# A hybrid decoder layer on one core: sums of weights' blocks moved in halves

## The chip, the cores and the metric

The kernel runs on one core of a Trainium2 chip. The metric is the device time of one execution in microseconds (us); less is better. Times come from repeated executions; the profile is of one of them.

## The reference

One decoder layer on 512 tokens of width 2048, in float32, cut to what matters:

```python
h = rmsnorm(x, g_pre)
q, k, v, z_att, u, g_glu, z_conv = split(h @ w_in, 7 * [1024])
y_att  = stick_breaking_attention(q, k, v) * silu(z_att)        # 8 heads of 128, causal
c = u * sigmoid(g_glu)
c = causal_depthwise_conv(c, conv_w, width=31) + conv_b
y_conv = (silu(layernorm(c)) @ w_pw2 + b_pw2) * silu(z_conv)
out = x + rmsnorm(concat(y_att, y_conv) @ w_out, g_post)
```

## The kernel before

Every product is made of three matmuls on parts: a float32 block is split on the chip into a rounded upper part (`h_...`, made by ScalarE, ACT) and a lower part (`l_...`, made by VectorE, DVE). The weights come from memory in blocks of one megabyte (`r_...`, two buffers), asked for on SyncE's queue (SP). TensorE (PE) follows an order written out by hand: a list of *steps*, each with one block of weights and mostly two *units* of 24 matmuls. The block of the next step is loaded while a step runs; its upper part, then its lower part, is made from it, and the lower part's end frees the buffer for another load.

The order of the steps, with the tiles' names: a prologue for the first gate columns (`gn`, in 16 blocks `n`); `u`, `q`, `k`, `g` of the first columns (steps 0 to 7); the values `v` (steps 8 to 21); the rest of `u`, `q`, `k`, `g`, with the attention heads in between, and the gates `za` (22 to 49); the gates `z` (50 to 63); the pointwise product `pw` (64 to 67); the output product `w` (68 to 95).

Three of the products, `v`, `z` and the output, use seven block products in place of eight. Four of the seven need a sum of blocks of the weights (5, 6, 7 and 4 in `SUMS`). These sums are not made on the chip's engines but in memory: `plan_sums` makes a list of transfers, each asked for on GpSimd's queue (POOL). For each sum two blocks per pair (`kg` 0 and 1; the output has two pairs `p`) are first copied into a tile in memory, out of the weights or out of an earlier finished sum (L528); then another block of the weights is added onto each by an accumulating transfer (L524). A block is 128 rows of 4 pieces of 2 KB. The tiles are `vs`, `zs` and `ws`. `v` and `z` have 16 transfers each, the output 32, 64 in all. SP later loads the finished sums like other weights.

The transfers are spread over the steps: `sum_next` takes the next of a list and ties it to the last matmul that was put down (`latest`), so it is not asked for before that matmul is done. POOL's queue is in order, so what stands behind a waiting request waits too. For `v`: one after every second block of the prologue from `n` 5 on, then one after each of three units of four. For `z` and the output together (`sumq`, the lists taken in turn): 1.5 a step from step 20 to 48, and again from step 64 on.

POOL also cuts off the future in the attention (`affine_select` on `t`, L698: four on each of two tiles per head, which the transposes `aT` wait for), clears the edge of `hg` (L401), adds up `ln_sum` and makes some products with gates. DVE makes the lower parts and, in the background, the 31 taps of the convolution (L410). ACT writes 16 pieces of prepared activations (`kept`) to memory for later.

Of the kernel before, what the change touches and what calls it, by code (L numbers as in the profile page):

```python
# [11 lines left out]
F32 = mybir.dt.float32  # L12
F32R = mybir.dt.float32r
AF = mybir.ActivationFunctionType
ALU = mybir.AluOpType

P = 128
S = 512
# [31 lines left out]
SUMS_FROM, SUMS_A_STEP = 20, 1.5  # L50
# [3 lines left out]
def hybrid_layer(  # L54
# [15 lines left out]
    nc = tc.nc  # L70
# [10 lines left out]
    dram = ctx.enter_context(tc.tile_pool(name="dram", bufs=1, space=bass.MemoryType.DRAM))  # L81
# [355 lines left out]
    def layer_norm():  # L437

        mu = mean_of(ln_sums[0], "mu")
        yield  # L440
        sqs = [late(f"ln_sq{c}") for c in range(CT)]
        for c in range(CT):
            nc.vector.tensor_tensor(out=conv[c], in0=conv[c], in1=mu, op=ALU.subtract)
            nc.scalar.activation(sqs[c], conv[c], AF.Square)
            if c >= 2:
                eng = nc.gpsimd if c % 2 == 0 else nc.vector
                eng.tensor_tensor(out=sqs[c % 2], in0=sqs[c % 2], in1=sqs[c], op=ALU.add)
            yield
        nc.vector.tensor_tensor(out=sqs[0], in0=sqs[0], in1=sqs[1], op=ALU.add)
        var = mean_of(sqs[0], "var")  # L450
        v, y, t = late("ln_v"), late("ln_y"), late("ln_t")
        nc.vector.tensor_scalar_add(v, var, LN_EPS)
        tc.keep_in_program_order(nc.scalar.preload_act_table_set(LN_EXP))
        rsqrt(y, v, t)
        yield
        for c in range(CT):
            nc.vector.tensor_tensor(out=conv[c], in0=conv[c], in1=y, op=ALU.mult)
            nc.scalar.activation(
                conv[c], conv[c], AF.Silu, scale=vec[:, c, V_LG : V_LG + 1],
                bias=vec[:, c, V_LB : V_LB + 1],  # L460
            )
            yield
        for c in range(CT):
            s_hi[c], s_lo[c] = late(f"s_hi{c}", F32R), t2(f"s_lo{c}", F32R)
            split(s_hi[c], s_lo[c], conv[c])
            yield
# [8 lines left out]
    def rows_first(ps, w, between):  # L475


        hi, lo = w
        parts = [h_at(i, 0, P) for i in range(4)]
        for n, (which, i) in enumerate(FIRST):  # L480
            a, b = {"hh": (0, hi), "hl": (0, lo), "lh": (1, hi)}[which]
            nc.tensor.matmul(
                ps, parts[i][a], b[:, i, :], start=n == 0, stop=False, skip_group_check=True
            )
            for f in between.get(n + 1, ()):
                f()

    def rows_block(kg, m, ps, w, between=()):

        hi, lo = w  # L490
        parts = [h_at(kg * 4 + i, m * P, (m + 1) * P) for i in range(4)]
        for i, (a, _) in enumerate(parts):
            nc.tensor.matmul(ps, a, hi[:, i, :], start=kg + i == 0, stop=False, skip_group_check=True)
            nc.tensor.matmul(ps, a, lo[:, i, :], start=False, stop=False, skip_group_check=True)
            if i == 0:
                for f in between:
                    f()
        for i, (_, a) in enumerate(parts):
            last = kg == 3 and i == 3
            latest[0] = nc.tensor.matmul(  # L500
                ps, a, hi[:, i, :], start=False, stop=last, skip_group_check=True
            ).ins
# [5 lines left out]

    SUMS = {5: ((0, 0), (0, 1)), 6: (5, (1, 1)), 4: (6, (1, 0)), 7: ((0, 1), (1, 1))}
    PLAIN = {1: (0, 0), 3: (1, 1), 2: (1, 0)}

    def plan_sums(name, order, pairs, block):

        made, todo = {}, deque()
        for q in order:
            base, more = SUMS[q]
            for accumulate in (False, True):
                for p in range(pairs):  # L520
                    for kg in range(2):
                        def go(q=q, base=base, more=more, accumulate=accumulate, p=p, kg=kg):
                            if accumulate:
                                return nc.gpsimd.dma_start(  # L524
                                    made[q, p, kg], block(*more, p, kg), accum_op=ALU.add
                                )
                            made[q, p, kg] = dram.tile([P, 4, S], F32, name=f"{name}{q}{p}{kg}")
                            return nc.gpsimd.dma_start(  # L528
                                made[q, p, kg],
                                made[base, p, kg] if isinstance(base, int)  # L530
                                else block(*base, p, kg),
                            )
                        todo.append(go)
        return made, todo

    def sum_next(todo):

        if todo:
            tc.add_manual_dep(
                todo.popleft()().ins, latest[0].name,  # L540
                mybir.DependencyInfo(mybir.DependencyClass.Sync, mybir.DependencyReason.DATA),
                reason="not before its step",
            )
# [12 lines left out]
    def v_w(r, c, p, kg):  # L556
        rows_ = slice((r * 2 + kg) * S, (r * 2 + kg + 1) * S)
        return w_in[rows_, C_V + c * S : C_V + (c + 1) * S].rearrange("(k p) c -> p k c", p=P)

    v_sum, v_sumq = plan_sums("vs", (5, 6, 7, 4), 1, v_w)  # L560
    v_form, v_ps, v_part = {}, {}, {}

# [404 lines left out]
    def load_final():  # L967
        for e in range(4):
            gp[e] = fin.tile([P, S], F32, tag="gp", bufs=4, name=f"gp{e}")
            nc.sync.dma_start(gp[e], g_post[e * S : (e + 1) * S].partition_broadcast(P))  # L970
# [243 lines left out]
    n_zc = len(steps)  # L1214
    gates_c()
    n_in = len(steps)
# [9 lines left out]
    with tc.manual_schedule(engines={mybir.EngineType.DVE, mybir.EngineType.Activation}):  # L1226
# [77 lines left out]
        def do(f, *args):  # L1304
            return partial(f, *args)
# [48 lines left out]
        for n, (kg, m) in enumerate(blocks):  # L1354
            if n == 0:
                rows_first(ps0[0], w0[0][1:], {8: [do(turn_block, 1)]})
            else:
                rows_block(
                    kg, m, ps0[m], w0[kg][1:], [do(turn_block, n + 1)] if n + 1 < len(blocks) else (),
                )  # L1360
            for f in plan[n]:
                f()
            if n + 1 < len(blocks):
                keeps[n + 1]()
            if n >= 5 and n % 2:
                sum_next(v_sumq)
        keep_rows(3)
        for _ in range(4):
# [36 lines left out]
    units_done, due = 0, 0  # L1405
    for n, step in enumerate(steps):
        if n == n_att:
            start.close()
            zp = att.enter_context(tc.tile_pool(name="zp", bufs=1, space=bass.MemoryType.PSUM))
            op = att.enter_context(tc.tile_pool(name="op", bufs=1, space=bass.MemoryType.PSUM))  # L1410
            attp = att.enter_context(tc.tile_pool(name="attp", bufs=1))
        if n == n_norm:
            att.close()
            conv_stack.close()
            op2 = ctx.enter_context(
                tc.tile_pool(name="op2", bufs=4, space=bass.MemoryType.PSUM)
            )
            late_stack = ExitStack()
            late_pool = late_stack.enter_context(tc.tile_pool(name="late", bufs=11))
            ln = layer_norm()  # L1420
            bgq.extend([lambda: next(ln, None)] * (3 * CT + 3))
        if n == n_pw - 1:
            make_form(ORDER[0])
        if n == n_pw:
            late_stack.close()
            fin = ctx.enter_context(tc.tile_pool(name="fin", bufs=1))
            load_final()
        if SUMS_FROM <= n < n_zc - 1 or n >= n_in:
            due += SUMS_A_STEP
        if n + 1 < len(steps) and n + 1 not in loaded:  # L1430
            loaded[n + 1] = steps[n + 1].load()
        w = loaded.pop(n)
        for unit in step.units:
            unit(w)
            units_done += 1
            if units_done % 4:
                sum_next(v_sumq)
            if due >= 1:
                sum_next(sumq)
                due -= 1  # L1440
            if n == 0 and unit is step.units[0]:
                turn_vectors()
            if n < n_norm:
                ticks[0] += 1
                next(heads_run)
                if n_v <= n < n_att:
                    background(1, LATER, weights_split[0])
                else:
                    background(4, LATER)
            else:  # L1450
                background(2, LATER)
# [28 lines left out]
```

## Time and profile before

| | |
|---|---|
| median of 3 runs | 857.09 us (856.87 to 857.32) |
| the profiled execution's own time, and its span | 858.71 us, 857.0 us |
| busy: PE, PEld, DVE, ACT, POOL | 847.6, 702.3, 658.5, 417.3, 137.6 us |
| DMA queue of SP (q1): MB, share of 16 engines | 120.74, 41.0% |
| DMA queue of POOL (q0): MB, share of 16 engines | 69.21, 33.7% |
| clock granted to PE | 0.998 |

The profile is taken inside one execution: the span runs from its first to its last instruction. PE is the matmul itself, PEld the load of its weights, which overlaps it. A matmul of 512 columns is listed with 0.39 us but the next starts 0.23 us after it, since they are pipelined; so short gaps do not show as idle. Where a row ends in brackets, the number is the engine's idle time before it, and behind the arrow stands what ended it. A DMA's time runs from the request to its landing.

### The profile page before, as it was taken

To read this page: it belongs to the slowest core of one execution; us is meant where nothing else is said; L and a number is where in the kernel's file an instruction comes from. 1 tells how busy PE (TensorE), PEld (TensorE's weight loads), DVE (VectorE), ACT (ScalarE), POOL (GpSimd) and SP (SyncE) were. 2 spreads that over 40 slices of the span, in tenths; PEclk is the share of its full clock that TensorE was granted. 3 is DMA by queue.
4 is the path that set the end of the run, shared out by engine and by line. 5 is a ranking of instruction groups with operands and counts; after the bars stand their busy time and mean duration, and the time that the engine had idled before them with its cause. 6 is when DMAs were issued, how large, how long until landed. Compare 5 with 4: busy or idle time off the path is not lost.

```text
span 857.0 us, 9935 instructions
## 1 busy us (share of the span) xinstructions
PE 847.6 (99%) x3872; PEld 702.3 (82%) x3872; DVE 658.5 (77%) x791; ACT 417.3 (49%) x475; POOL 137.6 (16%) x170
## 2 busy tenths in 40 slices
PE   9999999999999999999999999999999999999996
PEld 7888878888888888888888888888888888888885
DVE  5698899777589798997969898468964776458774
ACT  6784222565534342436432535369843356455543
POOL 0111110010130223222121333330000100000031
PEclk9999999999999999999999999999999999999999
DMA  8798989575877879876689887937755995557783
GB/s 317 243 289 196 325 256 234 191 225 196 299 229 209 245 148 215 276 197 196 191 222 188 235 245 159 283 103 289 295 197 197 220 263 205 197 197 260 288 282 102
DMA packets 92278, 195.04 MB, mean 228 GB/s; under 512 B 3702, under 2 KB 46210, under 8 KB 86856
## 3 DMA queue, kind: packets, MB, share of 16 engines
q1 hardware_dynamic: 66688, 120.74, 41.0%
q0 software_dynamic: 22304, 69.21, 33.7%
q10 hardware_dynamic: 3240, 4.46, 1.5%
q8 instruction: 30, 0.49, 0.2%
q14 instruction: 16, 0.13, 0.0%
HBM read 186.01 MB, written 75.50 MB: 305 GB/s over the span
## 4 chain that ended last, share of the span: by engine, by line
PE 91%; DMA 4%; DVE 2%; ACT 2%; issue 0%; POOL 0%; ACTq 0%; DVEq 0%; POOLq 0%
PE za L351 3%; PE za L353 3%; PE a L1089 3%; PE za L352 3%; PE a L1090 3%; PE a L1091 3%; PE k L353 3%; PE k L351 3%; PE k L352 3%; PE u L351 3%; PE u L353 3%; PE u L352 3%; PE q L353 3%; PE q L351 3%; PE q L352 3%; DMA r_q<-in_w_in_dram 2%
## 5 line engine op out<-in xcount | busy, mean ns | idle before, releaser
L410 DVE SCALAR_TENSOR_TENSOR acc<-hg,vec,acc 128x512 f32<-128x512 f32 x240 | 183.1, 763 | 7.2
L105 DVE TENSOR_TENSOR l_w<-r_w,h_w 128x2048 fp32r<-128x2048 f32 x28 | 64.2, 2292 | 43.5 <-ACT h_w L104 43.5
L104 ACT ACTIVATE h_w<-r_w 128x2048 fp32r<-128x2048 f32 x28 | 53.6, 1916 | 43.4 <-DMA r_w<-ws 16.9
L353 PE MATMUL k<-h_hi,l_k 128*128 128x512 f32 x128 | 50.0, 390 | 1.1 <-DVE l_k L105 1.1
L351 PE MATMUL u<-h_hi,h_u 128*128 128x512 f32 x128 | 50.1, 392 | 0.0
L351 PE MATMUL q<-h_hi,h_q 128*128 128x512 f32 x128 | 50.1, 392 | 0.0
L351 PE MATMUL za<-h_hi,h_za 128*128 128x512 f32 x128 | 50.1, 391 | 0.0
L351 PE MATMUL k<-h_hi,h_k 128*128 128x512 f32 x128 | 50.1, 391 | 0.0
L353 PE MATMUL q<-h_hi,l_q 128*128 128x512 f32 x128 | 49.9, 390 | 0.0
L353 PE MATMUL za<-h_hi,l_za 128*128 128x512 f32 x128 | 49.9, 390 | 0.0
L353 PE MATMUL u<-h_hi,l_u 128*128 128x512 f32 x128 | 49.9, 390 | 0.0
L352 PE MATMUL u<-h_lo,h_u 128*128 128x512 f32 x128 | 49.8, 389 | 0.0
L352 PE MATMUL za<-h_lo,h_za 128*128 128x512 f32 x128 | 49.8, 389 | 0.0
L352 PE MATMUL q<-h_lo,h_q 128*128 128x512 f32 x128 | 49.8, 389 | 0.0
L352 PE MATMUL k<-h_lo,h_k 128*128 128x512 f32 x128 | 49.8, 389 | 0.0
L1091 PE MATMUL a<-h_w,f_lo 128*128 128x512 f32 x128 | 49.8, 389 | 0.0
L1089 PE MATMUL a<-h_w,f_hi 128*128 128x512 f32 x128 | 49.8, 389 | 0.0
L1090 PE MATMUL a<-l_w,f_hi 128*128 128x512 f32 x128 | 49.8, 389 | 0.0
L105 DVE TENSOR_TENSOR l_z<-r_z,h_z 128x2048 fp32r<-128x2048 f32 x14 | 32.1, 2291 | 16.3 <-ACT h_z L104 16.3
L105 DVE TENSOR_TENSOR l_v<-r_v,h_v 128x2048 fp32r<-128x2048 f32 x14 | 32.1, 2290 | 15.3 <-ACT h_v L104 15.3
L698 POOL TENSOR_SCALAR_AFFINE_SELECT t<-t 128x128 f32<-128x128 f32 x64 | 33.6, 562 | 54.1 <-ACT t L734 30.1
L104 ACT ACTIVATE h_v<-r_v 128x2048 fp32r<-128x2048 f32 x14 | 26.8, 1916 | 29.6 <-PE g L352 13.2
(381 smaller groups left out, 2238.2 us busy)
## 6 DMA issues: line engine op xcount, KB each, us to landing
ws<-in_w_out_dram POOLq DMA_DIRECT2D x24, 1024.0 KB, 9.4
r_w<-ws SPq DMA_DIRECT2D x16, 1024.0 KB
vs<-in_w_in_dram POOLq DMA_DIRECT2D x12, 1024.0 KB, 12.7
zs<-in_w_in_dram POOLq DMA_DIRECT2D x12, 1024.0 KB, 9.3
r_w<-in_w_out_dram SPq DMA_DIRECT2D x12, 1024.0 KB
r_u<-in_w_in_dram SPq DMA_DIRECT2D x8, 1024.0 KB
r_q<-in_w_in_dram SPq DMA_DIRECT2D x8, 1024.0 KB
r_k<-in_w_in_dram SPq DMA_DIRECT2D x8, 1024.0 KB
```

The costliest lines, as they stand in the source:

```text
L104: nc.scalar.activation(hi, src, AF.Copy)
L105: made = nc.vector.tensor_tensor(out=lo, in0=src, in1=f32(hi), op=ALU.subtract)
L351: nc.tensor.matmul(ps, wh, ah, start=first, stop=False)
L352: nc.tensor.matmul(ps, wh, al, start=False, stop=False)
L353: latest[0] = nc.tensor.matmul(ps, wl, ah, start=False, stop=last).ins
L410: bgq.append(lambda j=j: nc.vector.scalar_tensor_tensor(out=acc, in0=hg[:, j : j + S], scalar=vec[:, ct, j : j + 1], in1=acc, op0=ALU.mult ...
L698: nc.gpsimd.affine_select(out=blk, in_=blk, compare_op=ALU.is_gt, fill=0.0, base=0, pattern=[[-1, P]], channel_multiplier=1,)
L1089: nc.tensor.matmul(ps, fh[:, kk, ts], hi[:, k, :], start=st, stop=False, skip_group_check=True)
L1090: nc.tensor.matmul(ps, fh[:, kk, ts], lo[:, k, :], start=False, stop=False, skip_group_check=True)
L1091: nc.tensor.matmul(ps, fl[:, kk, ts], hi[:, k, :], start=False, stop=en, skip_group_check=True)
```

## The change

Each transfer that makes sums of weights moves half a block (two of the four pieces of each row), so there are 128 in place of 64; a copy and the addition onto it are halved alike, and a tile is made with its first half. They are asked for twice as often: for `v`, after each block of the prologue from 5 on (11 halves, where there were 6 wholes), then two after the first unit and one after the second, in turn; for `z` and the output, 1.5 halves a unit in place of 1.5 blocks a step. The bytes are the same, the loads of the finished sums as well, and no other line differs.

```diff
-                    for kg in range(2):
-                        def go(q=q, base=base, more=more, accumulate=accumulate, p=p, kg=kg):
+                    for kg, half in ((0, 0), (0, 1), (1, 0), (1, 1)):
+                        def go(q=q, base=base, more=more, accumulate=accumulate, p=p, kg=kg, half=half):
+                            ks = slice(2 * half, 2 * half + 2)
                             if accumulate:
                                 return nc.gpsimd.dma_start(
-                                    made[q, p, kg], block(*more, p, kg), accum_op=ALU.add
+                                    made[q, p, kg][:, ks], block(*more, p, kg)[:, ks],
+                                    accum_op=ALU.add,
                                 )
-                            made[q, p, kg] = dram.tile([P, 4, S], F32, name=f"{name}{q}{p}{kg}")
-                            return nc.gpsimd.dma_start(
-                                made[q, p, kg],
-                                made[base, p, kg] if isinstance(base, int)
-                                else block(*base, p, kg),
-                            )
+                            if half == 0:
+                                made[q, p, kg] = dram.tile([P, 4, S], F32, name=f"{name}{q}{p}{kg}")
+                            src = made[base, p, kg] if isinstance(base, int) else block(*base, p, kg)
+                            return nc.gpsimd.dma_start(made[q, p, kg][:, ks], src[:, ks])
...
-            if n >= 5 and n % 2:
+            if n >= 5:
                 sum_next(v_sumq)
...
-        if SUMS_FROM <= n < n_zc - 1 or n >= n_in:
-            due += SUMS_A_STEP
...
             units_done += 1
-            if units_done % 4:
+            for _ in range(1 + units_done % 2):
                 sum_next(v_sumq)
-            if due >= 1:
+            if SUMS_FROM <= n < n_zc - 1 or n >= n_in:
+                due += SUMS_A_STEP
+            while due >= 1:
                 sum_next(sumq)
                 due -= 1
```

## The prediction

> **What bounds the kernel now.** I read the page's busy line and then the waits of TensorE (PE).
>
> ```profile
> span 857.0 us, 9935 instructions
> PE 847.6 (99%) x3872; PEld 702.3 (82%) x3872; DVE 658.5 (77%) x791; ACT 417.3 (49%) x475; POOL 137.6 (16%) x170
> PE idle L1283 <- POOL mean_w L140: 1.8, 1, 1.8
> PE last L1159 <- ACT diag L1158: 1.5, 1, 1.5
> PE k L353 <- DVE l_k L105: 1.1, 1, 1.1
> ```
>
> PE is busy for 99% of the span, and of its three waits (us in total, times, longest) one lies before any weight is used and one at the very end. Only the third, 1.1 us of the `k` products on a lower part `l_k`, lies where weights come from memory. The transfers that the change touches write blocks that nothing but PE's weights are made from, so all that they can give back is that 1.1 us. What they can cost is not so bounded. The windows say where the time of PE stands:
>
> ```profile
> 60.00:140.00 80.00, 78.86 (x357) 64.72 (x356) 71.17 (x100) 25.20 (x29) 10.20 (x12) 1.00 0.96 264
> 140.00:215.00 75.00, 75.00 (x331) 61.63 (x330) 58.74 (x56) 37.96 (x38) 2.97 (x2) 1.00 0.64 208
> 215.00:560.00 345.00, 345.00 (x1619) 289.36 (x1618) 283.88 (x304) 146.91 (x124) 93.35 (x124) 1.00 0.82 223
> ```
>
> After the length come PE, PEld, DVE, ACT and POOL, then the granted clock, the DMA share and GB/s. Between 60 and 140 us the DMA engines are 0.96 busy and PE loses 1.1 us; from 140 to 560 it loses nothing. The chain in order of time (start, length) shows what ends last in the crowded stretch:
>
> ```profile
> 70.78 19.23 DMA r_q<-in_w_in_dram
> 92.52 2.30 DVE l_q L105
> 94.84 18.96 DMA r_k<-in_w_in_dram
> 113.90 1.93 ACT h_k L104
> 115.85 2.31 DVE l_k L105
> 118.20 0.50 PE k L353
> ```
>
> A weight load takes 19 us here, the next may start only when `l_q` has freed its buffer, and PE waits for the second. How thin the room is on the way is told by the timelines of DVE and PE:
>
> ```profile
> 94.72 8.62 DVE L410 SCALAR_TENSOR_TENSOR acc<-hg,vec,acc 128x512 f32<-128x512 f32 x11
> 103.27 2.28 DVE L105 TENSOR_TENSOR l_k<-r_k,h_k 128x2048 fp32r<-128x2048 f32 x1
> 108.31 6.25 DVE L410 SCALAR_TENSOR_TENSOR acc<-hg,vec,acc 128x512 f32<-128x512 f32 x8
> 115.85 2.29 DVE L105 TENSOR_TENSOR l_k<-r_k,h_k 128x2048 fp32r<-128x2048 f32 x1 [1.29 <-ACT h_k L104]
> 95.19 0.39 PE L353 MATMUL q<-h_hi,l_q 128*128 128x512 f32 x1
> 106.08 0.39 PE L353 MATMUL k<-h_hi,l_k 128*128 128x512 f32 x1
> ```
>
> The first `l_k` is done at 105.55 (103.27 + 2.28) and first used at 106.08: 0.53 us to spare. One step earlier, at 95.19 (106.08 less two units of 5.44 us, see below), the second `l_q` is first used; it was done at 94.82: 0.37 to spare. The second `l_k` has none. DVE had finished its taps at 114.56 (108.31 + 6.25) and idled 1.29 us for that load, so if the load came 1.29 us sooner, `l_k` would end 1.29 sooner and the 1.1 us wait of PE would be gone.
>
> **The change, part by part.** (1) *The pace of the `v` sums.* POOL's timeline gives the present requests in that stretch:
>
> ```profile
> 67.15 1.18 POOL L524 DMA_DIRECT2D vs<-in_w_in_dram  x1 [6.01 <-PE u L353]
> 73.45 1.16 POOL L524 DMA_DIRECT2D vs<-in_w_in_dram  x1 [5.12 <-PE u L353]
> 78.89 0.75 POOL L528 DMA_DIRECT2D vs<-in_w_in_dram  x1 [4.28 <-PE u L353]
> 89.77 0.73 POOL L528 DMA_DIRECT2D vs<-in_w_in_dram  x1 [10.13 <-PE q L353]
> 95.21 1.18 POOL L524 DMA_DIRECT2D vs<-in_w_in_dram  x1 [4.71 <-PE q L353]
> 100.65 1.17 POOL L524 DMA_DIRECT2D vs<-in_w_in_dram  x1 [4.25 <-PE q L353]
> 111.52 0.53 POOL L528 DMA_DIRECT2D vs<-vs  x1 [9.71 <-PE k L353]
> ```
>
> One whole block after three of every four units (a unit is 5.44 us, 95.21 to 100.65). The new loops ask for 11 halves in the first stage where 6 wholes were asked, then for 2, 1, 2, 1 halves a unit: the same 3 wholes in 4 units, half a block to a whole block later. Counted from the code in wholes: by 73.5 us 8 were asked for and now 7, by 95.2 us 11 and now 10, by 100.7 us 12 and now 11, by 111.5 us 13 and now 12.5. Of what shares the engines with the second `r_k` (94.84 to 113.80), the first accumulating block moves from 95.21 to about 100.7 and the second from 100.65 to about 106 and 111.5.
>
> What a block in flight costs a load: a megabyte alone is bounded from above by the median landing of a copy, 6.4 us (`ws<-ws`, next fence). The second `r_k` took 18.96 with a copy and two accumulating blocks beside it, so 12.6 us for at most three, 4 us or more each. One accumulating block that starts 5.4 us later takes away at most those 4 us and at least nothing (if something else is in its place by then). 1.29 is needed, a third of the price of one block. I take the whole 1.1 us: **minus 1.1 us**, ends 0 and minus 1.1. The load after it, `r_g`, then meets the accumulating half that came late; `l_g` is what is late next, and up to the half block's 2 us could return there.
>
> (2) *Issue time on POOL.* From the view of the tile `vs` (ns, least, median, most) and the page's issues:
>
> ```profile
> L524 POOL DMA_DIRECT2D vs<-in_w_in_dram x8: 1158/1178/1215, 40.4 to 134.7; - x8
> L528 POOL DMA_DIRECT2D vs<-in_w_in_dram x4: 707/726/754, 27.6 to 89.8; - x4
> L528 POOL DMA_DIRECT2D vs<-vs x4: 499/516/526, 53.7 to 124.8; - x4
> L639 SPq DMA_DIRECT2D r_v<-vs x8: 319/329/349, 160.4 to 209.9; - x8
> DMA to landing us min/median/max: 5.9/10.7/15.9
> ws<-ws POOLq DMA_DIRECT2D x8, 6.4
> ```
>
> All three sums together make 32 accumulating blocks, 16 copies out of the weights and 16 copies of a finished sum (`vs` is a quarter): 32 x 1.178 + 16 x 0.726 + 16 x 0.516 = 57.6 us. A half costs at least half of that (sum +0) and at most as much as a whole (sum +57.6). The copy of one contiguous block, 0.516, is nearest to a fixed part; with half of the rest on top an accumulating half takes 0.85, a copying half 0.62. A half of a finished sum is no longer contiguous but 128 rows of 4 KB; I put it between 0.516 and 0.62, at 0.57. That is 64 x 0.85 + 32 x 0.62 + 32 x 0.57 = 92.5 us, **+35 us of POOL**, from 138 to some 172 us busy, 20% of the span. None of it is on PE's path while the masks of the attention, which POOL makes behind these requests, keep their room:
>
> ```profile
> 318.74 3.45 POOL L698 TENSOR_SCALAR_AFFINE_SELECT t<-t 128x128 f32<-128x128 f32 x4 [11.14 <-DVE t L721]
> 327.54 2.56 POOL L698 TENSOR_SCALAR_AFFINE_SELECT t<-t 128x128 f32<-128x128 f32 x4 [4.24 <-ACT t L734]
> 331.75 1.09 PE aT L742 x10
> 533.64 1.03 POOL L698 TENSOR_SCALAR_AFFINE_SELECT t<-t 128x128 f32<-128x128 f32 x4 [5.64 <-ACT t L734]
> 536.23 1.09 PE aT L742 x10
> ```
>
> The masks end at 330.10 and 534.67, their transposes start at 331.75 and 536.23: 1.65 and 1.56 us of room. Before the change a whole's request could stand in front of a mask for at most 1.2 us; now one or two halves can, 1.70 us at most, so 0.5 us more. Both masks keep about 1 us: **0 us**, up to +0.14 where two halves fall right before the thinner one and it had none in front (1.70 less 1.56).
>
> (3) *New waits.* Each new request waits for the last product of its unit and stands in POOL's queue; behind it wait masks, the memory clears for `hg` and the sums `ln_sum`. The requests of finished sums come at the same distance behind their parts as before, in blocks, two to three units (10.9 to 16.3 us) after them, where the median landing is 10.7; a later landing holds POOL's queue and nobody in it is due yet. **0 us.** (4) *Later ends.* The last half of `v` is asked for one unit later, at about 140 us and not at 134.7; the loads of finished sums (`r_v<-vs`) run from 160.4 to 209.9, those of the last sum at the end. The 48 `z` and `w` blocks keep 3 halves a step where they had 1.5 blocks: **0 us**. (5) *Bytes* are the same; pieces of 4 KB in place of contiguous megabytes, in 16 copies of 64, are below what I can price: **0 us**, between minus and plus a microsecond in the stretch of point 1.
>
> **Sum.** The profiled execution took 858.71 us, 1.6 more than the median of 857.09. 858.71 - 1.1 = 857.6; less the same 1.6 that is **856.0**.
>
> **Rivals.** *A, each half pays its own fixed cost, and the loads slip.* Should two halves occupy the engines a fifth longer than a whole, a load that lost 12.6 us to its neighbours loses 2.5 more. The second `r_q` has 0.37 us of room, so PE stops 2.1 us for it; the second `r_k` starts 2.5 later and is 2.5 slower again, which adds 2.5. 857.1 + 4.6 = 861.7 us. It is slower by over 0.2% once the new stalls reach 1.7 us, that is from about 8% (two loads each 1.04 us longer, less 0.37, are 1.7). For it: the DMA share of 0.96. Against: the requests fall behind by half a block to one block in the same place.
> The Trainium skill, page "DMA: Bandwidth & Descriptors", section on the anatomy of one SWDGE transfer, speaks for A: about 2.0 us fixed plus bytes over 436 GB/s. By its figures a whole is 4.4 us and two halves 6.4, an estimate of 45% more, which would put this rival near 868 us. By the same section most of the fixed part is the wait for the receipt of the last write, a latency and not work of the engines; no row here shows that split, so the chance of A stays as it is.
> *B, a mask is held up.* If POOL's order puts a half that still waits for its unit in front of a mask, the mask is late by up to a unit: 5.44 - 1.65 = 3.8 us at one head, 856.0 + 3.8 = 859.8. For it: twice as many waiting requests on the same queue. Against: the waits of POOL before these masks (11.14 on DVE, 4.24 and 5.64 on ACT) are for the masks' own inputs.
> *C, the load is no faster.* Another block stands in the way of `r_k`, or the gain comes back at `l_g`: 857.1 us.
>
> **How the numbers follow.** About 0.2% (1.7 us) is what can be told from no change here. Forecast 0.54 (855.4 to 856.6), C 0.24 (856.6 to 858.8), A 0.10, B 0.07, and 0.05 for a gain whose source the profile does not show. Same is the forecast and C, 0.78; slower is A and B, 0.17; faster is the 0.05, since the only wait that can go is smaller than the bound. The range runs from 855.3 (the wait and the fraction of a microsecond that repeated runs differ by) to 859.0, which leaves out most of A and the upper part of B.
>
> **What would show it.** Right: the wait of `k` on `l_k` gone from PE's list, the second `r_k` in under 17.7 us, POOL 165 to 180 us busy, requests of 0.85, 0.62 and 0.57 us, transposes `aT` without a wait. Wrong: a wait of `q`, `k` or `g` on its lower part between 90 and 135 us (A, or C at `l_g`), a wait of `aT` on POOL (B), or requests as long as the wholes' (+58 us of POOL).

## The result and the profile after

The changed kernel is slower: 870.99 us (median of 6 runs, 867.88 to 873.95) against 857.21 us, a ratio of 1.0157 with a 95% interval of 1.013 to 1.0184. The prediction was 856.0, within 855.3 to 859.0. Here and below ratios are of fast runs alone, which leaves out one execution of 1848 us of the experiment `e5`; some runs of the kernel before took 860 to 864 us and are in, so that a ratio can lie up to 0.2% below that of the medians. The profiled execution took 870.32 us. Busy times and the waits of PE, from the page and from the view of waits (us in total, times, longest):

```profile
span 868.6 us, 10048 instructions
PE 851.6 (98%) x3872; PEld 703.3 (81%) x3872; DVE 658.2 (76%) x791; ACT 416.4 (48%) x475; POOL 189.0 (22%) x234
PE ln_mu L433 <- ACT mu_hi L104: 4.2, 1, 4.2
PE ln_mu L434 <- DVE mu_lo L105: 1.7, 1, 1.7
PE va L663 <- DVE l_v L105: 1.4, 1, 1.4
PE g L353 <- DVE l_g L105: 0.9, 1, 0.9
PE k L353 <- DVE l_k L105: 0.4, 1, 0.4
```

The wait of `k` that the prediction counted, at the second `l_k`, is gone (the 0.4 us are at the first), but `g` and `va` wait in its place, and two new waits, 5.9 us together, stand where the prediction had not looked: at the products `ln_mu` of the layer norm's mean, near 560 us. The windows of the changed kernel, and the last of them in the kernel before:

```profile
60.00:140.00 80.00, 78.67 (x352) 63.84 (x351) 67.68 (x95) 24.59 (x28) 18.37 (x22) 1.00 1.01 264
140.00:215.00 75.00, 73.40 (x322) 59.82 (x321) 59.95 (x60) 36.98 (x37) 4.10 (x3) 1.00 0.68 208
215.00:560.00 345.00, 343.39 (x1611) 287.76 (x1609) 277.75 (x295) 142.19 (x117) 120.64 (x163) 1.00 0.90 217
560.00:650.00 90.00, 85.72 (x366) 70.36 (x367) 69.76 (x69) 65.02 (x76) 12.95 (x9) 0.96 0.62 225
```

```profile
560.00:650.00 90.00, 90.00 (x398) 74.42 (x397) 69.00 (x67) 63.90 (x69) 7.36 (x5) 1.00 0.59 213
```

Where in the span the time goes is told by the first and last start (last two numbers ahead of the semicolon, us) of the products of one tile. First the changed kernel, then the kernel before in a second profiled execution of 857.22 us (below, `e12`):

```profile
L663 PE MATMUL va<-l_v,h_hi x32: 387/389/497, 151.4 to 229.5; 128*128 128x512 f32 x32
L353 PE MATMUL za<-h_hi,l_za x128: 388/389/628, 479.9 to 583.5; 128*128 128x512 f32 x128
```

```profile
L662 PE MATMUL va<-l_v,h_hi x32: 387/389/390, 149.3 to 225.3; 128*128 128x512 f32 x32
L353 PE MATMUL za<-h_hi,l_za x128: 388/389/398, 475.6 to 570.6; 128*128 128x512 f32 x128
```

The changed kernel is 2.1 us late at the first value, 4.2 at the last, still 4.3 at the first gate `za`, and 12.9 at the last. So two pieces have to be explained: 4.2 us in the crowded first stage, and 8.6 us inside the gates. The second piece is one chain; from the chain in order of time (start, length) of the changed kernel:

```profile
537.56 21.45 DMA r_za<-in_w_in_dram
...
559.12 1.92 ACT h_za L104
...
563.27 1.76 DVE mu_lo L105
...
565.08 0.79 PE ln_mu L434
565.87 0.43 PE za L351
...
569.60 0.23 PE za L351
```

The last gate load takes 21.45 us; in the kernel before it took 8.0 (worked out from the trace, request at 533.14 to landing at 541.10). The mean does not use it, but on ACT its upper part stands ahead of the upper part of the mean's input, as the timeline shows (changed kernel, then the kernel before in its first profile, as in all timelines below):

```profile
559.12 1.91 ACT L104 ACTIVATE h_za<-r_za 128x2048 fp32r<-128x2048 f32 x1 [12.83 <-DMA r_za<-in_w_in_dram]
561.87 0.64 ACT L104 ACTIVATE mu_hi<-ln_sum 128x512 fp32r<-128x512 f32 x1
```

```profile
548.07 1.92 ACT L104 ACTIVATE h_za<-r_za 128x2048 fp32r<-128x2048 f32 x1 [4.55 <-PE za L352]
550.83 0.64 ACT L104 ACTIVATE mu_hi<-ln_sum 128x512 fp32r<-128x512 f32 x1
```

Before, `h_za` waited for PE; after, it waits 12.83 us for the load, and `mu_hi` with it. After that pause the matmuls start 0.43 us apart instead of 0.23, from 565.87 to 569.60: nine at 0.43 (the last of them shorter) cost some 1.7 us more, which the windows show as a granted clock of 0.96 behind 560 us. The Trainium skill ("TensorE: Matmul & The Clock Gate", section "What's actually happening") says that one idle window of about 3.4 us halves the clock and that about 3.4 us of work restores it; the 3.7 us at half pace agree.

### The profile page after: what moved, and what is told of

The parts are those of the page before. It is cut to its first block, busy times and chain, and to the rows that moved or that the text cites. A ratio compares the mean times of both kernels' runs of the same rounds, so it can differ in the third digit from the quotient of the medians.

```text
span 868.6 us, 10048 instructions
## 1 busy us (share of the span) xinstructions
PE 851.6 (98%) x3872; PEld 703.3 (81%) x3872; DVE 658.2 (76%) x791; ACT 416.4 (48%) x475; POOL 189.0 (22%) x234
## 4 chain that ended last, share of the span: by engine, by line
PE 81%; DMA 10%; DVE 5%; ACT 2%; issue 1%; POOL 0%; ACTq 0%; DVEq 0%; POOLq 0%
PE a L1091 3%; PE a L1092 3%; PE a L1090 3%; PE u L351 3%; PE u L352 3%; PE u L353 3%; DMA r_k<-in_w_in_dram 3%; PE za L352 3%; PE za L351 3%; PE za L353 3%; PE k L351 3%; PE q L351 3%; PE q L353 3%; PE k L353 3%; PE q L352 3%; PE k L352 3%
## 5 line engine op out<-in xcount | busy, mean ns | idle before, releaser
L526 POOL DMA_DIRECT2D ws<-in_w_out_dram x32 | 38.2, 1249 | 72.8 <-PE u L353 18.1
```

Of the source, the lines that this page charges most:

```text
L526: return nc.gpsimd.dma_start(made[q, p, kg][:, ks], block(*more, p, kg)[:, ks], accum_op=ALU.add,)
```

## The experiments

Each was measured against the kernel before on the chip that it ran on itself (medians of 857.19 to 857.47 us). "Old" and "new" pace are the moments of the kernel before and of the changed one.

**Pace or halves.** `e1`: the changed kernel, halves asked for in pairs at the old moments. `e2`: whole blocks at the moments of the second halves.

```diff
 # e1, and likewise at the two other places
-            if n >= 5:
+            if n >= 5 and n % 2:
                 sum_next(v_sumq)
+                sum_next(v_sumq)
 # e2, with whole blocks
-                        todo.append(go)
+                        todo.extend((None, go))      # nothing at a first half's moment
```

> Halves as in the changed kernel, but both halves of a block are asked for at the point where the kernel before asked for the whole block. Theory S (the splitting costs: a half's request holds POOL 1.15 us against 1.17 for a whole, and a half lands after a median of 9.1 us against 9.4): slower than before by 6 to 14 us, POOL near 189 us busy, a wait of ln_mu on mu_hi or waits of q, k, g, v on their lower parts. Theory P (the new moments of the requests do it): within 2 us of before, only the 1.1 us wait of k, POOL still near 189.

> Whole blocks, each asked for at the moment at which the changed kernel asks for the block's second half; nothing at the first half's. Theory S: within 1.5 us of before (perhaps 1 us faster, since the second r_k meets its neighbours later), POOL near 138 us. Theory P: slower by 6 to 14 us as the changed kernel, with the ln_mu wait.

`e1` took 872.55 us (1.0181, 1.0166 to 1.0196), `e2` 858.26 (1.0002, 0.9989 to 1.0016). The new pace costs at most a microsecond; the halves are what costs. In `e2` a transpose waits for a mask (its row among the waits of PE, and the mask in POOL's timeline):

```profile
PE aT L744 <- POOL t L700: 0.7, 1, 0.7
535.14 1.02 POOL L700 TENSOR_SCALAR_AFFINE_SELECT t<-t 128x128 f32<-128x128 f32 x4 [5.06 <-ACT t L736]
```

This is not rival B: POOL idled 5.06 us before that mask, for the mask's own input from ACT, and no request stood in front of it.

**Which sums, which transfers.** `e3` halves `v` alone, `e4` `z` and the output alone (the others whole, at the old pace); `e5` keeps additions whole and halves copies, `e6` the reverse.

```diff
 # e3
-    z_sum, z_sumq = plan_sums("zs", (5, 6, 4, 7), 1, z_w)
+    z_sum, z_sumq = plan_sums("zs", (5, 6, 4, 7), 1, z_w, True)   # whole
 # e5: HALVED = (False,), e6: HALVED = (True,)
+                            whole = accumulate not in HALVED
+                            ks = slice(0, 4) if whole else slice(2 * half, 2 * half + 2)
```

> Halves and new moments for the v sums alone; z and w sums whole at the old moments. The changed kernel lies 2.8 us behind before at 215 us (first u load after the values at 218.06 against 215.29) and 11.5 behind at the pointwise product. If the two stages are independent: plus 2.8 us, with waits of g and v on their lower parts and no ln_mu wait. If the early lag alone brings the later stall about: plus 6 to 14.

> Halves and new moments for the z and w sums alone; v sums whole at the old moments. Independent stages: plus 8 to 9 us, with the ln_mu wait of 6 us followed by matmuls at half pace, and the 1.1 us wait of k as before. If the early lag is needed for the later stall: within 2 us of before.

> The changed kernel with its 32 additions as whole blocks (each asked for where its second half was), only the copies in halves. Theory F (a finished sum's copy goes in 4 KB pieces where it was contiguous, 64 KB a piece, and that crowds the weight loads): slower than before by 8 to 14 us. Theory G (two halves of an addition in flight together crowd the loads): within 3 us of before. Theory R (the requests' time on POOL): half the extra requests, plus 3 to 8 us.

> The changed kernel with its 32 copies as whole blocks, only the additions in halves. Theory F: within 3 us of before. Theory G: plus 8 to 14 us, mean weight load between 215 and 560 us above 10 us (7.9 before, 12.0 changed). Theory R: plus 3 to 8 us.

`e3` 859.80 us (1.0032), `e4` 869.24 (1.0142), `e5` 858.13 (1.0003, 0.9989 to 1.0018), `e6` 869.09 (1.0121, 1.0084 to 1.0157). `e3` and `e4` (2.5 and 12.0 us by the medians) add up to about the whole loss, and the copies do not cost: a finished sum copied in 4 KB pieces, the prediction's step 5, is free. It is the additions.

**Requests or pieces.** `e7` keeps the 128 requests and their moments, but a half is 64 rows with all four pieces, one contiguous stretch of 512 KB. `e8` has whole blocks at the new pace and two extra clears on POOL for each first half.

```diff
 # e7
-                            ks = slice(2 * half, 2 * half + 2)
+                            ks = slice(64 * half, 64 * half + 64)    # of rows, [ks] for [:, ks]
 # e8
+    def hold():      # two nc.gpsimd.memset of 128x512, tied to `latest` like a request
```

> As the changed kernel, same moments, same 128 requests, but a half is 64 rows with all four pieces, so each half of a finished sum is contiguous (512 KB). Theory F: back to within 3 us of before. Theories G and R: plus 8 to 14 us as the changed kernel.

> Whole blocks at the second halves' moments (which cost nothing, 858.26 against 857.28 us), and at each first half's moment two clears of a spare 128x512 tile on POOL tied to the same matmul, about 0.5 us each: 64 times about 1 us of POOL time without a transfer. Theory R: plus 6 to 14 us. Theories F and G: within 2 us of before, POOL near 195 us busy.

`e7` 859.07 us (1.0005, 0.9984 to 1.0026), `e8` 858.04 (0.999, 0.9971 to 1.0009), with POOL busier than in the changed kernel:

```profile
PE 847.3 (99%) x3872; PEld 702.0 (82%) x3872; DVE 659.2 (77%) x791; ACT 417.0 (49%) x475; POOL 200.3 (23%) x298
```

So neither POOL's time nor the number of requests costs more than the 1.6 us by which the median of `e7` lies above 857.45. I read `e7` as "the gaps in the pieces cost all of it", which turned out half right.

**The gaps, and the place.** `e9` is the changed kernel with a tile of its own, contiguous, for each half; what is read stays two pieces of each row. `e10` is the changed kernel without requests in steps 46 to 48, ahead of the mean.

```diff
 # e9
+made[q, p, kg] = dram.tile([2, P, 2, S], F32, name=f"{name}{q}{p}{kg}")   # [half] for [:, ks]
 # e10
-            if SUMS_FROM <= n < n_zc - 1 or n >= n_in:
+            if SUMS_FROM <= n < n_zc - 4 or n >= n_in:
```

> The changed kernel with one thing different: the two halves of a sum's block get their own 512 KB of memory each, so that what a half writes is one contiguous stretch, and not 128 stretches of 4 KB with gaps of 4 KB. What it reads of the weights (two of the four 2 KB pieces of each of 128 rows), the number of requests and their moments stay; the loads of finished sums read 4 KB stretches in place of 8 KB. Theory 'gaps in what is written': additions that write with gaps are what slows the loads beside them; here the time falls to 857 to 860 us, the wait of ln_mu (5.9 us in the changed kernel) is under 1 us, the mean weight load between 215 and 560 us takes about 8.5 us as with halves by rows. Theory 'pieces that are read': the choice of two pieces of each row in the source is what costs; the time stays at 867 to 873 us, ln_mu waits 4 us or more.

> The changed kernel, but no half of z or w is asked for in the steps 46 to 48 (PE's 520 to 553 us); the nine halves come after 645 us with the others that were left over. Theory 'ACT's queue': the 8.8 us at the mean of the normalization come from the sums beside the last gate load (it took 21.45 us), since the upper part of the mean's input stands behind h_za in ACT's queue. Then ln_mu waits under 1.5 us in place of 5.9, the slow matmuls behind that wait go too, and the time is 861 to 864 us. Rival 'a debt from before': the loads are late from what was asked for up to 520 us, and the wait stays at 4 us or more, with 868 us or more.

`e9` 865.48 us (1.0098, 1.0083 to 1.0114): between the two theories. Its first stage lost nothing (`va` first at 149.8 us), but it still waited 3.8 and 1.7 us at `ln_mu`. `e10` 870.69 us (1.0159): the wait of `ln_mu` is gone, as its theory had it, and the time did not move, which no theory had. The nine halves that were put off run beside the loads of the output product, which now come late instead:

```profile
PE a L1090 <- ACT h_w L104: 5.3, 1, 5.3
PE a L1091 <- DVE l_w L105: 1.5, 1, 1.5
PE b L1091 <- DVE l_w L105: 1.0, 1, 1.0
```

**The predicted gain.** `e11` has whole blocks and moves the `v` sums alone to the new pace; `e12` is the kernel before, unedited, profiled again.

```diff
 # e11
-                        todo.append(go)
+                        todo.extend((None, go) if name == "vs" else (go,))
```

> The kernel before with whole blocks throughout; only the sums of v are asked for at the moments of the changed kernel's second halves, those of z and w at the old ones. Theory 'the pace of v alone is the gain that the prediction saw': the wait of k on l_k (1.1 us) is gone and, unlike with all sums moved, no transpose aT waits for a mask (0.7 us there); 856.1 us, that is 0.9985 to 0.9990 of before. Rival 'it comes back elsewhere': a wait of g or v takes its place and the time is that of before, within 0.3 us.

> The kernel before without any edit, profiled a second time. The prediction took the 1.1 us wait of k on l_k from one execution that lasted 858.71 us, 1.6 us above the median of the others; with that wait gone in the profile (whole blocks, the v sums later) the median did not fall. Theory 'an accident of one execution': the second profile shows the wait of k under 0.4 us and a span of 855.3 to 856.1 us. Rival 'the wait is always there and its gain is eaten elsewhere': the wait stands again between 0.8 and 1.4 us, in a span of 855.3 to 857.

`e11` 857.38 us (1.0001, 0.9992 to 1.001), with no wait of `k`, `g` or `v` in its profile. `e12` shows why nothing was gained. Its span, and all its waits of PE:

```profile
span 855.5 us, 9935 instructions
PE idle L1283 <- POOL mean_w L140: 1.8, 1, 1.8
PE last L1159 <- ACT diag L1158: 1.5, 1, 1.5
```

The 1.1 us wait of `k` is absent: it belonged to the one execution that had been profiled, 1.6 us over the median. What the later requests do to the load behind it can be seen all the same: the second `r_k` takes 19.1 us in `e12`, 16.6 in `e11` and 21.4 in the changed kernel (worked out from the traces).

**Gaps without the pieces.** `e13` is the kernel before with sums that lie in memory as 4 KB stretches with gaps of 4 KB, as in the changed kernel (the 8 KB of the texts below are from one start to the next); `e14` is `e7` with the same. Both also load finished sums with gaps, which the changed kernel does not.

```diff
-made[q, p, kg] = dram.tile([P, 4, S], F32, name=f"{name}{q}{p}{kg}")
+made[q, p, kg] = dram.tile([P, 2, 4, S], F32, name=f"{name}{q}{p}{kg}")[:, :, 0:2]
```

> The kernel before (whole blocks at their old moments), but the blocks of the sums lie in memory as 256 stretches of 4 KB with gaps of 8 KB between them, so that additions, copies and loads of finished sums all meet gaps; requests, bytes and what is read of the weights stay. Theory 'gaps alone': what the changed kernel pays for what it writes with gaps it pays with whole blocks as well; some 861 to 866 us, with additions of over 13 us to landing (10.6 before). Theory 'gaps only double a half': a whole with gaps has 512 pieces to move as before and lands as before; 857 to 859 us.

> Halves by rows (64 rows, all four pieces; 859.07 us), at the same moments, with blocks that lie in memory as 4 KB stretches with gaps of 8 KB. Theory 'gaps cost a half its speed': additions land in about 10 us as by pieces (8.4 by rows without gaps), the time is 863 to 870 us. Theory 'it is the reading of two pieces of every row': additions land in 8.4 us or a little more, 858.5 to 861 us.

`e13` 879.81 us (1.0265, 1.0231 to 1.0299), `e14` 871.76 (1.016, 1.0129 to 1.019). Additions slow down without any halving: whole ones land in 13.2 us in the median where they took 10.6, halves by rows in 10.1 where they took 8.4. Not all of the time is theirs: both wait at late loads of finished sums (`a` on `l_w`, 3.4 and 3.2 us), where no sum is in flight. Yet `e14` has no wait at `ln_mu`, though its additions are as slow as the changed kernel's. So slow additions alone do not make the mean wait.

**The order on ACT.** It stands in ACT's timeline. The changed kernel, then the kernel before:

```profile
491.81 1.27 ACT L735 ACTIVATE t<-t 128x1280 f32<-128x1280 f32 x1 [6.74 <-DVE t L734]
492.98 1.90 ACT L104 ACTIVATE h_za<-r_za 128x2048 fp32r<-128x2048 f32 x1
```

```profile
487.53 1.92 ACT L104 ACTIVATE h_za<-r_za 128x2048 fp32r<-128x2048 f32 x1 [5.24 <-PE za L352]
489.35 1.26 ACT L734 ACTIVATE t<-t 128x1280 f32<-128x1280 f32 x1
```

PE's order is written by hand; the order on the other engines is laid out when the kernel is built. With 128 requests in the program it came out with the third split `h_za` behind an exponential of head 6, which waits for DVE. I call this the swap, or the changed kernel's order. DVE's timeline shows what follows (same two kernels):

```profile
494.92 2.29 DVE L105 TENSOR_TENSOR l_za<-r_za,h_za 128x2048 fp32r<-128x2048 f32 x1 [3.20 <-ACT h_za L104]
...
535.26 2.27 DVE L105 TENSOR_TENSOR l_za<-r_za,h_za 128x2048 fp32r<-128x2048 f32 x1
```

```profile
489.48 2.29 DVE L105 TENSOR_TENSOR l_za<-r_za,h_za 128x2048 fp32r<-128x2048 f32 x1 [0.55 <-ACT h_za L104]
...
530.84 2.28 DVE L105 TENSOR_TENSOR l_za<-r_za,h_za 128x2048 fp32r<-128x2048 f32 x1
```

DVE idles 3.20 us in place of 0.55 and then works without a pause until the split that frees the buffer for the last gate load. That split ends at 537.53, not 533.12: 4.4 us later, of which 2.8 are the kernel's own delay by then (the first `za` at 479.9, not 477.1). The load starts later by as much. The profiles of all kernels so far that lost time at the mean (`e1`, `e4`, `e6`, `e9` and the changed one) have the swap, and in all of them the last gate load took 21 to 22 us. `e2`, `e5`, `e8` and `e10` have the swap too, but there this load took 7.7 to 11.4 us and the mean did not wait; the others lack the swap. So `e7` against the changed kernel had compared two orders as well as two ways of halving. Three kernels set the order by hand: `e15` the changed kernel in the old order, with no other difference on ACT, DVE and SP and one on POOL, where one request for a `ws` block stands ahead of a mask and not behind it; `e16` the halves by rows in the new order; `e17` `e9` in the old order.

```diff
+                tc.add_manual_dep(exps[6], gate_his[2].name, ...)   # e16: the two exchanged
```

> The changed kernel with one swap in ACT's queue: the split h_za of the third gate load stands ahead of the exponential of head 6 again, as in the kernel before; in the changed kernel it stands behind it (492.98 and not about 489.6 us). Everything else in the queues is as in the changed kernel. Theory 'order': the 8.7 us at the mean need this swap, which the build made by itself; they go, and the time is 861 to 864 us, with the losses before 305 us left. Rival 'the additions alone': ln_mu still waits 4 us or more, 868 us or more.

> Halves by rows (859.07 us), with that split put behind the exponential as in the changed kernel. Theory 'order alone': the swap costs its 8 us with any halves, and the time is 865 to 869 us. Theory 'order and slow additions together': with halves by rows the loads are quick enough to bear it, and the time is 858 to 861 us (whole blocks with other work on POOL had this order and lost 0.9 us at the mean).

> Halves by pieces with targets of their own (865.48 us), with that split ahead of the exponential as in the kernel before. Theory 'order': that kernel lost time at the mean alone, so this one is at 857 to 858.5 us: halves by pieces cost nothing once the target has no gaps and the order is the old one. Rival 'what is read by pieces costs': 864 us or more.

| us (ratio) | order of the changed kernel | order of the kernel before |
|---|---|---|
| halves by pieces, into a tile with gaps | 870.99 (1.0157), the change | 863.66 (1.007, 1.0042 to 1.0097), `e15` |
| halves by pieces, contiguous tiles | 865.48 (1.0098), `e9` | 857.58 (1.0003, 0.9994 to 1.0013), `e17` |
| halves by rows, contiguous | 861.48 (1.0052), `e16` | 859.07 (1.0005), `e7` |
| whole blocks | 858.26 (1.0002), `e2`; 858.04 (0.999), `e8` (with clears) | 857.38 (1.0001), `e11` (new pace for `v` alone) |

With halves by pieces the order (with that one request) is worth 7.3 us (870.99 less 863.66) with gaps and 7.9 without, the gaps 5.5 in the new order and 6.1 in the old. The four kernels of the first two rows differ in their engines' queues by nothing else, but 4 to 6 runs of those that lose time spread over as much as 6 us, so these prices are good to some 3 us. With both undone, 128 transfers by pieces cost nothing. In the new order whole blocks pay 0.7 us or less at a transpose and nothing at the mean. `e16` is not clean: it waits not for `mu_hi` but for a mask,

```profile
PE aT L747 <- POOL t L703: 2.3, 1, 2.3
```

and the swap by hand had moved another activation (`sz`) forward there. The gates in `e15`, `e9` and `e17`, first to last product:

```profile
L357 PE MATMUL za<-h_hi,l_za x128: 388/389/628, 478.0 to 578.4; 128*128 128x512 f32 x128
```

```profile
L353 PE MATMUL za<-h_hi,l_za x128: 387/389/628, 476.1 to 579.1; 128*128 128x512 f32 x128
```

```profile
L357 PE MATMUL za<-h_hi,l_za x128: 387/389/398, 475.5 to 570.8; 128*128 128x512 f32 x128
```

They take 100.4, 103.0 and 95.3 us, where the kernel before takes 95.0 and the changed one 103.6. In `e15`'s profiled execution (865.18 us, its runs lie between 861.21 and 866.17) the mean still waited 3.3 us, while its last value started at 226.5 us, only 1.2 late where the changed kernel was 4.2 late with the same queues up to there: single executions can differ by 3 us there.

What makes the swap dear is the last gate load. ACT's timeline has its split in `e17`, and in `e16`, where the swap cost no wait at the mean:

```profile
548.32 1.92 ACT L106 ACTIVATE h_za<-r_za 128x2048 fp32r<-128x2048 f32 x1 [6.43 <-DMA r_za<-in_w_in_dram]
```

```profile
549.17 1.92 ACT L106 ACTIVATE h_za<-r_za 128x2048 fp32r<-128x2048 f32 x1 [3.28 <-PE za L356]
```

In every kernel that halves the additions for `z` and the output by pieces, except `e10`, this load takes 18.5 to 22 us, with gaps or without and in either order (21.9 in `e15`, 18.5 in `e17`); by rows it takes 5.8 to 7.8 (`e16`, `e7`, `e14`). At some 20 us the stretch is at its limit, and the gaps and the order each move it over; at 8 us it bears either, as `e14` the gaps and `e2` and `e5` the swap. Why it is long by pieces stays open: the kernels by rows also have another order of requests, masks and products on POOL there, and no run has one without the other.

How slow an addition is stands in the view of its line: request on POOL (ns, least, median, most), and landing for all additions of the kernel. Before, changed, `e17`:

```profile
L524 POOL DMA_DIRECT2D zs<-in_w_in_dram x8: 1156/1177/1196, 245.9 to 457.0; - x8
DMA to landing us min/median/max: 9.0/10.6/15.9
```

```profile
L526 POOL DMA_DIRECT2D zs<-in_w_in_dram x16: 1135/1170/1632, 245.2 to 467.8; - x16
DMA to landing us min/median/max: 6.4/10.0/15.0
```

```profile
L530 POOL DMA_DIRECT2D zs<-in_w_in_dram x16: 1035/1058/1561, 240.6 to 463.3; - x16
DMA to landing us min/median/max: 6.3/8.9/14.0
```

Half the bytes are 10.0 us in flight where all of them took 10.6, so more additions run beside each weight load. From issue to landing the weight loads between 215 and 560 us took 12.0 us in the mean in the changed kernel, 9.7 in `e17` and 7.9 before (worked out over all 29 or 30 loads of that stretch). Why writing with gaps holds an addition up is not shown. The time that the packets of the sums take on the 16 engines does not tell it either: it is 36.4% of the span in `e5`, which loses 0.7 us at most, and 36.1% in `e6`, which loses 11.6.

## Why the prediction was wrong

*The sum's only term, minus 1.1 us.* With whole blocks the load did get quicker with the `v` sums later (19.1 to 16.6 us, `e12` and `e11`), but there was nothing to gain: the wait was in one execution, which was 1.6 us too long, and taking off first its 1.1 us and then the 1.6 took the same excess off twice. The term was worth nothing that shows (`e12`, `e11`).

*Step 2, POOL.* Requests of 0.85, 0.62 and 0.57 us were predicted; in the medians for `vs` they took 1.154, 0.690 and 0.535. The time to make a request hardly falls with its bytes, so POOL gained 51.4 us (137.6 to 189.0), not 35, still inside the bounds of 0 and 57.6. That none of it is on the path held (`e8`).

*Step 5, pieces.* Put at 0, within a microsecond, it is the term that was mis-sized. I looked at the 16 copies of finished sums, which are free (`e5`), and not at the 64 additions, each of which now writes 128 stretches of 4 KB with gaps: 5.5 to 6.1 us.

*Step 4, later ends.* The `z` and output sums, at 3 halves a step for 1.5 blocks, were put at 0. They are where most of it was lost: `e4`, which halves them alone, takes 12.0 us more. Their halves run beside the gate loads, and the last of these took 21.45 us, not 8.0.

*What had no step.* 7.3 us go away when an order is set back that the diff does not touch: the build chose it anew on ACT. By itself it costs a microsecond at most (`e2`, `e5`); dear it is only with a gate load of some 20 us. The prediction took every other instruction to stay where it was, and took 140 to 560 us as safe because PE lost nothing there. That a window is 100% busy says that its waits are covered, not by how much. The question to ask was which instruction waits behind a load in its engine's queue without needing it: `mu_hi` behind `h_za`.

*Rival A* (each half pays its own cost, the loads slip) was given 0.10. Its signs came: waits at `g` and at the loads after it, landings of a half almost as long as a whole's. But its place, the first loads and the values behind them, holds only 4.2 of the 12.9 us in the profile, and its cause is not the fixed cost of a transfer. By the figures of the Trainium skill ("DMA: Bandwidth & Descriptors", anatomy of one SWDGE transfer) it stood near 868 us, three from the measured time; `e17` has the same 128 transfers and takes 857.58, so the agreement was chance. The section's other point, that most of the fixed part is a wait for the receipt of the last write, fits `e17`; no run here shows the receipt itself. *Rival B* was not seen: PE waits for no mask in the changed kernel, and the mask of `e2` was late for another reason. *Rival C*, no gain, is the state of `e11`.

## What to carry to other kernels

When an accumulating transfer from memory to memory is cut up, cut it so that each part writes one contiguous stretch. By rows was the safer way here (859.07 and 861.48 us in the two orders); into a tile of its own it took 857.58 in one and 865.48 in the other. Before a wait is priced as a gain, profile a second execution and look whether it is there. And when a change adds many instructions, compare the queues of all engines afterwards, not only the lines of the diff: an order that the build lays out can change far from the edit, and a swap that costs nothing while the load behind it is quick (8 us) costs several microseconds once it takes 20.

## What was not expected of the hardware

An addition of a whole block slows by a quarter (10.6 to 13.2 us to landing) when the sums lie in memory with gaps and the requests stay as they were (`e13`, where copies and loads of the sums meet the gaps too). The time that POOL takes to issue an addition follows the shape more than the bytes: in the medians for `zs` 1177 ns for a contiguous megabyte, 1170 for half of it into a tile with gaps, 1058 into a tile of its own, 975 by rows, 1434 for a whole with gaps. And two waits of PE, of 4.2 and 1.7 us with one matmul between them, cost some 1.7 us more in matmuls at half pace behind them.
